# Three edits of an order in an encoder layer: feature casts of the first FFN step put later, an event for each half of the residual's spill, eleven dummy matmuls

## The chip, the cores and the metric

The kernel runs on one core of one Trainium2 chip. The metric is the device time of one execution in microseconds; the time before is the median of three runs. One further execution was taken with the hardware profiler, and all readings of the trace are from that one.

## The reference, cut to what matters

One encoder layer over 256 tokens of width 2048. What bears on the change is the middle of it:

```python
h  = h + rms_norm(mixed, g_mix_post)
fn = rms_norm(h, g_ffn_pre)
ff = (silu(fn @ w_ffn_gate) * (fn @ w_ffn_up)) @ w_ffn_down      # 2048 -> 5632 -> 2048
h  = h + rms_norm(ff, g_ffn_post)
gate = sigmoid(rms_norm(h, g_ple_pre) @ w_ple_gate)
h  = h + rms_norm(gate * (p @ w_ple_proj), g_ple_post)
```

Ahead of it stand one input projection, neighbourhood attention for half of the columns, a two-way recurrence for the other half, and an output projection.

## The kernel before, in words

**Products.** Each float32 operand is split into a high part (a cast to a reduced type) and a low part (the operand less its high part), and a product is three matmuls: high by high, low by high, high by low. A weight tile is 256 rows by 512 columns, one load of 512 KB into a raw tile (`wr`, `third`, `lower`). ScalarE casts it to `wh` (line 630), VectorE writes `wl` as the difference (line 643), and TensorE then runs twelve matmuls with the pair (lines 677 to 679). There are four `wh`/`wl` pairs in a ring (`W_BUFS = 4`), and in the FFN every fifth tile has a pair of its own, named `w`. A cast into a ring pair has to wait until TensorE is done with the tile that was there four ring casts earlier.

**FFN.** The 5632 columns are done in eleven steps `f` of 512, in three parts. In a step, the products with `w_ffn_gate` and `w_ffn_up` are formed (nine steps of the eleven, and most down products, do part of them with seven block products in place of eight, which needs sums of weight blocks made on VectorE at lines 578, 582 and 588, and one accumulating load on GpSimd's queue at line 599). `gate_post` writes silu of the gate to `mid`; `up_post` multiplies by the up product, transposes blocks on VectorE (line 334), and `moved` turns the tile by 16 small transfers `mT<-mid` (line 344). When these have landed, `carried` splits `mT` into the features `mid0h` and `mid0l` (lines 306 and 308) that the down products will read, and `mid_sums` makes block differences of `mT` in place (line 1761) and splits them into `sums`. The first step's features are first read after four steps.

**Combination.** When a group's seven block products are done, `made_of_four` joins them: a copy `u<-acc` on ScalarE (line 736), four subtractions on VectorE (lines 738 to 745), a copy `acc<-u` on ScalarE (line 730). The next group's matmuls add to these accumulators and wait for it.

**Residual.** `h` lies in two tiles of 1 MB, one for each half of the tokens. Once the FFN's input features exist, `spill_h` stores both to memory, so that their room can hold other tiles (`lower` in the first half's, `sums` in the second half's), and `reload` brings them back near the end.

**Order.** Every engine works through its instructions in the order in which they are written. That order comes from a planner at build time: each piece of side work is a generator that yields operations with an estimated cost. The planner keeps an estimated clock for each engine and takes, between the matmuls, the operation that can start first, with a lateness added or taken off. `plan.add(gen, ready, late)` starts a generator at the estimated time `ready`; an `Event` that a generator yields holds it until the estimated time of `done(event)`, which is `plan.now`. A new estimate moves instructions only where it changes which operation is taken first.

**Start.** `WARM` dummy matmuls of 128 columns on a tile of ones run on TensorE ahead of the first product (line 2101). Each is two records in the trace.

Of the kernel before, what the change touches and what calls it, by code (L numbers as in the profile page):

```python
# [18 lines left out]
NT = S // P  # L19
# [50 lines left out]
SOON = 2.0  # L70
ADDED = 6.0
AHEAD = 5
ISSUE = 160
WARM = 9


class Event:


    t = None  # L80
# [141 lines left out]
def dve(n, take=None, give=None):  # L222
    return ("dve", COST["dve"] + 0.00104 * n, None, take, give)
# [6 lines left out]
def dma(kb, take=None):  # L230
    return ("dma", kb / 340.0, None, take, None)
# [3 lines left out]
def layer(ctx: ExitStack, tc: tile.TileContext, a: dict, out: bass.AP):  # L235
# [5 lines left out]
    plan = Plan(wr=R_BUFS, w=W_BUFS, sm=SM_BUFS, acc=4, ev=1, mid=2, bt=2, m2=1, mt=1, sq=1, T0=1, T1=1, T4=1, **{f"{s}{j}": n for s, m, n in (("p", 5, 1), ("t", 3, 0)) for j in range(m)}, wr0=1, w0=1)  # L241
# [4 lines left out]
    def bank(name):  # L246
        return ps.tile([P, 2, S], F32, tag="sm", name=name, bufs=SM_BUFS)
# [55 lines left out]
    def split(hi, lo, src, n, give=None):  # L303

        yield act(n)
        nc.scalar.copy(hi, src)
        yield dve(n, give=give)
        nc.vector.tensor_tensor(out=lo, in0=src, in1=f32(hi), op=ALU.subtract)
# [19 lines left out]
    def moved(e, here, take, tile_of, turn=True, pool=()):  # L328


        if turn:
            flat = e.rearrange("p t n -> p (t n)")
            yield dve(2 * N)
            nc.vector.transpose(out=flat, in_=flat)
        src = e.rearrange("p t (k j b) -> p t k j b", j=4, b=32)
        mT = None
        for j in range(4):
            for i in range(4):
                first = None if mT else take
                yield ("pool" if i in pool else "dma", COST["move"], None, first, None)  # L340
                if mT is None:
                    mT = tile_of()
                dst = mT.rearrange("p t k (i b) -> p t k i b", b=32)
                (nc.gpsimd if i in pool else nc.sync).dma_start(  # L344
                    dst[32 * j : 32 * j + 32, :, :, i, :],
                    src[32 * i : 32 * i + 32, :, :, j, :],
                )
        done(here)
        return mT.rearrange("p t k q -> p k t q")

    def by_tile(v):
        return v.rearrange("p k (t q) -> p k t q", t=NT)
# [13 lines left out]
    def done(event):  # L366
        event.t = plan.now
# [438 lines left out]
    ev_unmerged = Event()  # L806
# [709 lines left out]
    def next_norm(sub, nxt, rstd, ev_rstd, g_next):  # L1516
# [51 lines left out]
        if sub is mix:  # L1568
            plan.add(spill_h(), plan.now)
# [28 lines left out]
        ).tile([NT, P, D], F32, name=f"part{i}")  # L1598
        for i in range(2)
    ]  # L1600
    ev_spilled, ev_back = Event(), Event()

    def spill_h():
        for e in hF.ev:
            yield e
        for t in range(NT):
            yield dma(1024)
            nc.sync.dma_start(spill[t], t2["h"].tiles[t])
        done(ev_spilled)

    half_spill = ctx.enter_context(
        tc.tile_pool(name="half_spill", bufs=1, space=bass.MemoryType.DRAM)
# [106 lines left out]
    def up_post(f, mid, kk0, g, soon):  # L1719

        def post(ch):
            yield g.free
            e = es.pop(f)
            for t in range(NT):
                yield dve(N)
                nc.vector.scalar_tensor_tensor(
                    out=e[:, t, :], in0=ch.accs[t], scalar=rstd_f[:, t : t + 1], in1=e[:, t, :],
                    op0=ALU.mult, op1=ALU.mult,
                )
            ch.release()  # L1730
            there = Event()
            mT = yield from moved(e, there, "mt", mT_tile, pool=(0, 2) if soon else range(4))
            plan.free["mid"].append(plan.now)
            yield there
            plan.add(carried(mid, kk0, mT), plan.now + (0.5 if soon else 3.0), -SOON if soon else 0.0)
        return post

    def carried(mid, kk0, mT):
        summed = any(kk0 <= kx < kk0 + 4 for kx in mid.ev_sums)
        for b in range(0, 4, 2):  # L1740
            kk = kk0 + b
            i, j = divmod(kk, 8)
            hi, lo = mid.tiles(i)
            yield from split(
                *(by_tile(x[:, j : j + 2, :]) for x in (hi, lo)), mT[:, b : b + 2], 2 * S,
                give="mt" if b and not summed else None,
            )
            mid.pair(kk)
        if summed:
            plan.add(mid_sums(mid, kk0, mT), plan.now + (20.0 if mid.name[-1] == str(2) else 0.0))  # L1750

    def mid_sums(mid, kk0, mT):

        yield ev_unmerged if kk0 else ev_spilled
        kxs = [kx for kx in DOWN_KS[2] if kk0 <= kx < kk0 + 4]
        m = 2 * len(kxs)
        a11, a12 = mT[:, 0:m:2, 0, :], mT[:, 1:m:2, 0, :]
        a21, a22 = mT[:, 0:m:2, 1, :], mT[:, 1:m:2, 1, :]
        for dst, x, y in ((a22, a21, a22), (a21, a21, a11), (a11, a11, a22), (a12, a12, a11)):
            yield dve(P * len(kxs))  # L1760
            nc.vector.tensor_tensor(out=dst, in0=x, in1=y, op=ALU.subtract)
        if kk0 == 0:
            if "sums" not in t2:
                t2["sums"] = t2["pool"].tile([P, 2, 4, S], F32R, tag="h1", name="sums")
            hi, lo = (by_tile(t2["sums"][:, i, :, :]) for i in range(2))
        else:
            hi, lo = (
                by_tile(t2["s"][:, 2 + i, :].rearrange("p (k s) -> p k s", s=S)) for i in range(2)
            )
        yield from split(hi, lo, mT[:, 0:m], m * S, give="mt")  # L1770
        for i, kx in enumerate(kxs):
            mid.sums[kx] = {
                n: tuple(x[:, 2 * i + k, t, :] for x in (hi, lo))
                for n, k, t in (("S2", 0, 0), ("S7", 0, 1), ("S4", 1, 0), ("S1", 1, 1))
            }
            done(mid.ev_sums[kx])
# [76 lines left out]
    for part, (f0, f1) in enumerate(PARTS):  # L1853
        mid = Mid(f"mid{part}")
# [243 lines left out]
    with tc.manual_schedule():  # L2098
        warm = bank("warm")
        for n in range(WARM):  # L2100
            nc.tensor.matmul(warm[:, 0, 0:P], ones, ones, start=True, stop=True)
# [90 lines left out]
```

## Time and profile before

| | |
|---|---|
| median of 3 runs | 1159.08 us (1156.46 to 1161.56) |
| the profiled execution's own time | 1159.04 us |
| its span, first to last instruction | 1157.1 us |
| TensorE busy | 1144.7 us (99% of the span) |
| VectorE, ScalarE, GpSimd busy | 903.7, 711.1, 133.5 us |
| mean granted TensorE clock | 0.997 |
| memory traffic | 222 GB/s over the span |

Times are in microseconds from the span's start unless marked ns. PE is TensorE, PEld its weight loads, DVE VectorE, ACT ScalarE, POOL GpSimd, SP SyncE, which issues most loads. A row of the timeline gives start, duration, engine, line, operation, output and inputs, count, and in brackets the engine's idle time before it and what ended that time. Ends of matmuls are modelled and overlap; the distance between two starts is the better measure of their pace. The granted clock is a share of full speed.

### The profile page before, as it was taken

What the parts mean: (1) busy time and instruction counts of PE and PEld (TensorE: products, weight loads), DVE (VectorE), ACT (ScalarE), POOL (GpSimd) and SP (SyncE); (2) the same over time, 40 slices, a digit from 0 to 9 for tenths busy, and PEclk for the clock granted to TensorE, in tenths of its full rate; (3) what the DMA queues carried; (4) which work ended last, traced back from release to release, by engine and by line L of the source; (5) the groups of instructions that cost most, each with busy time, mean ns of one, the idle gap of its engine ahead of it and who ended that gap; (6) DMA issues with size and microseconds to landing.
All of it is one profiled execution on the core that took longest, in us unless ns stands there. A gap on an engine that the chain in (4) does not pass through costs nothing.

```text
span 1157.1 us, 15105 instructions
## 1 busy us (share of the span) xinstructions
PE 1144.7 (99%) x5213; PEld 949.7 (82%) x5213; DVE 903.7 (78%) x1133; ACT 711.1 (61%) x944; POOL 133.5 (12%) x214
## 2 busy tenths in 40 slices
PE   9999999999999989999999999999999999999997
PEld 8888888888888878888888888888888888787886
DVE  6678787888468758898877898978878887868575
ACT  7777777875557545565555556555455564655664
POOL 0000000000000032131110133212111303100000
PEclk9999999999999999999999999999999999999999
DMA  9867666545686977877876877776987787875671
GB/s 323 286 186 226 183 180 206 179 158 200 224 283 189 307 197 260 241 228 231 249 246 219 261 220 216 258 246 205 316 260 252 217 265 241 271 239 198 221 247 75
DMA packets 112285, 266.39 MB, mean 230 GB/s; under 512 B 39248, under 2 KB 46160, under 8 KB 110800
## 3 DMA queue, kind: packets, MB, share of 16 engines
q1 hardware_dynamic: 99568, 243.57, 61.9%
q0 software_dynamic: 12208, 21.51, 9.5%
q8 instruction: 41, 0.67, 0.2%
q10 hardware_dynamic: 432, 0.35, 0.1%
q14 instruction: 36, 0.29, 0.1%
HBM read 247.55 MB, written 9.44 MB: 222 GB/s over the span
## 4 chain that ended last, share of the span: by engine, by line
PE 93%; DMA 3%; DVE 1%; ACT 1%; POOL 1%; issue 1%; ACTq 0%; DVEq 0%
PE acc L678 24%; PE acc L679 24%; PE acc L677 24%; PE acc L690 5%; PE acc L689 5%; PE acc L688 5%; DMA mT<-mid 3%; PE tr L325 1%; POOL mT L344 1%; DMA wr<-in_w_ffn_gate 1%; DVE wl L643 0%; PE pg L356 0%; PE pg L357 0%; PE pg L355 0%; DVE h L1548 0%
## 5 line engine op out<-in xcount | busy, mean ns | idle before, releaser
L643 DVE TENSOR_TENSOR wl<-wr,wh 128x1024 fp32r<-128x1024 f32 (+1 forms) x309 | 369.7, 1210 | 117.0 <-ACT wh L630 113.5
L630 ACT CAST wh<-wr 128x1024 fp32r<-128x1024 f32 (+1 forms) x309 | 320.3, 1043 | 197.0 <-PE acc L678 142.7
L678 PE MATMUL acc<-wh,hT_mix_lo 128*128 128x512 f32 x400 | 155.8, 390 | 0.3 <-DVE hT_mix_lo L314 0.3
L677 PE MATMUL acc<-wh,hT_mix_hi 128*128 128x512 f32 x400 | 155.9, 390 | 0.0
L679 PE MATMUL acc<-wl,hT_mix_hi 128*128 128x512 f32 x400 | 155.6, 389 | 0.0
L344 POOL DMA_DIRECT2D mT<-mid x152 | 89.4, 599 | 555.3 <-DMA wr<-in_w_ffn_gate 400.9
L679 PE MATMUL acc<-wl,hT_hi 128*128 128x512 f32 x320 | 124.5, 390 | 0.0
L677 PE MATMUL acc<-wh,hT_hi 128*128 128x512 f32 x316 | 124.4, 394 | 0.0
L678 PE MATMUL acc<-wh,hT_lo 128*128 128x512 f32 x316 | 123.1, 390 | 0.0
L630 ACT CAST wh<-ple 128x1024 fp32r<-128x1024 f32 (+1 forms) x57 | 56.4, 992 | 76.4 <-DVE ple L582 42.9
L678 PEld LDWEIGHTS acc<-wh,hT_mix_lo 128*128 128x128 f32 x400 | 75.1, 188 | 16.5 <-DVE hT_mix_lo L314 1.0
L679 PEld LDWEIGHTS acc<-wl,hT_mix_hi 128*128 128x128 f32 x400 | 75.1, 188 | 15.6
L677 PEld LDWEIGHTS acc<-wh,hT_mix_hi 128*128 128x128 f32 x400 | 75.1, 188 | 15.5
L643 DVE TENSOR_TENSOR wl<-ple,wh 128x1024 fp32r<-128x1024 f32 (+1 forms) x57 | 65.3, 1147 | 13.0 <-ACT wh L630 12.5
L679 PEld LDWEIGHTS acc<-wl,hT_hi 128*128 128x128 f32 x320 | 60.1, 188 | 12.9
L678 PEld LDWEIGHTS acc<-wh,hT_lo 128*128 128x128 f32 x316 | 59.4, 188 | 11.5
L677 PEld LDWEIGHTS acc<-wh,hT_hi 128*128 128x128 f32 x316 | 59.4, 188 | 11.5
L599 POOL DMA_DIRECT2D ple<-in_w_ffn_up x27 | 24.0, 890 | 172.5 <-DVE wl L643 124.6
L643 DVE TENSOR_TENSOR wl<-third,wh 128x1024 fp32r<-128x1024 f32 x31 | 37.8, 1219 | 5.5 <-ACT wh L630 5.5
L630 ACT CAST wh<-third 128x1024 fp32r<-128x1024 f32 x31 | 32.6, 1051 | 14.8 <-PE acc L678 10.0
L678 PE MATMUL acc<-wh,hT_ffn_lo 128*128 128x512 f32 x104 | 40.8, 393 | 0.5 <-DVE hT_ffn_lo L314 0.5
L677 PE MATMUL acc<-wh,hT_ffn_hi 128*128 128x512 f32 x104 | 40.8, 392 | 0.0
(439 smaller groups left out, 2457.3 us busy)
## 6 DMA issues: line engine op xcount, KB each, us to landing
wr<-in_w_ffn_gate SPq DMA_DIRECT2D x78, 512.0 KB, 5.5
wr<-in_w_in SPq DMA_DIRECT2D x77, 512.0 KB, 4.4
wr<-in_w_ffn_down SPq DMA_DIRECT2D x62, 512.0 KB, 5.5
wr<-in_w_ffn_up SPq DMA_DIRECT2D x48, 512.0 KB, 5.2
wr<-in_w_out SPq DMA_DIRECT2D x32, 512.0 KB, 4.3
wr<-in_w_ple_gate SPq DMA_DIRECT2D x32, 512.0 KB, 4.5
lower<-in_w_ffn_up SPq DMA_DIRECT2D x22, 512.0 KB, 6.2
third<-in_w_ffn_down SPq DMA_DIRECT2D x14, 512.0 KB, 5.4
```

The lines of the kernel that those rows point to most:

```text
L325: nc.tensor.transpose(tr[:, b, t * P : (t + 1) * P], e[:, t, sl], ident)
L344: (nc.gpsimd if i in pool else nc.sync).dma_start(dst[32 * j : 32 * j + 32, :, :, i, :], src[32 * i : 32 * i + 32, :, :, j, :],)
L599: nc.gpsimd.dma_start(dst, src, accum_op=ALU.add)
L630: nc.scalar.copy(his[i][:, 0 : src.shape[1], :] if n == 2 else his[i][:, j, :], src)
L643: nc.vector.tensor_tensor(out=los[i][:, m, :], in0=src, in1=f32(his[i][:, m, :]), op=ALU.subtract)
L677: nc.tensor.matmul(accs[t], hi[:, sl], his[i][:, j, :], start=st, stop=False, **group)
L678: nc.tensor.matmul(accs[t], lo[:, sl], his[i][:, j, :], start=False, stop=False, **group)
L679: nc.tensor.matmul(accs[t], hi[:, sl], los[i][:, j, :], start=False, stop=sp, **group)
L688: nc.tensor.matmul(dst, x[0], wh, start=start, stop=False, skip_group_check=seeded)
L689: nc.tensor.matmul(dst, x[1], wh, start=False, stop=False, skip_group_check=seeded)
L690: nc.tensor.matmul(dst, x[0], wl, start=False, stop=stop, skip_group_check=seeded)
```

## The change

Three edits. The 12.0 stands for the first FFN step only (`f` is 0); the other steps keep 3.0, and the last step of a part 0.5. `ev_spilled` now becomes done at the first half's spill, and `ev_all_spilled`, for which the first step's `mid_sums` waits, at the second's.

```diff
-WARM = 9
+WARM = 11
...
     def spill_h():
         for e in hF.ev:
             yield e
-        for t in range(NT):
+        for t, ev in enumerate((ev_spilled, ev_all_spilled)):
             yield dma(1024)
             nc.sync.dma_start(spill[t], t2["h"].tiles[t])
-        done(ev_spilled)
+            done(ev)
+            plan.now += 40.0 if t == 0 else 0.0
...
-            plan.add(carried(mid, kk0, mT), plan.now + (0.5 if soon else 3.0), -SOON if soon else 0.0)
+            plan.add(carried(mid, kk0, mT), plan.now + (0.5 if soon else 3.0 if f else 12.0), -SOON if soon else 0.0)
...
-        yield ev_unmerged if kk0 else ev_spilled
+        yield ev_unmerged if kk0 else ev_all_spilled
```

ScalarE's order in the second FFN step, where the first step's features `mid0h` and `sums` are made between casts of weight tiles; before:

```order
L630 CAST w<-wr 128x1024
L630 CAST wh<-third 128x1024
L306 CAST mid0h_3779<-mT 128x512 x2
L630 CAST wh<-ple 128x1024
L630 CAST wh<-wr 128x1024 x2
L630 CAST w<-wr 128x1024
L306 CAST sums<-mT 128x1024
L630 CAST wh<-wr 128x1024
```

The same place of the same engine in the changed kernel:

```order
L630 CAST w<-wr 128x1024
L630 CAST wh<-third 128x1024
L630 CAST wh<-ple 128x1024
L630 CAST wh<-wr 128x1024 x2
L630 CAST w<-wr 128x1024
L630 CAST wh<-wr 128x1024
L306 CAST mid0h_3781<-mT 128x512
L630 CAST wh<-third 128x1024
L306 CAST mid0h_3781<-mT 128x512
L630 CAST wh<-ple 128x1024
L306 CAST sums<-mT 128x1024
```

The first `mid0h` now stands behind five more weight casts, the second behind six, and `sums` behind three more. VectorE's order moves with it.

ScalarE near the end of the third FFN step, where `u<-acc` and `acc<-u` are the combination's copies; before:

```order
L630 CAST wh<-third 128x1024
L630 CAST wh<-wr 128x1024 x2
L736 COPY u<-acc_4194 128x512
L630 CAST wh<-wr 128x1024
L730 COPY acc_4195<-u 128x512
```

The same place of the same engine in the changed kernel:

```order
L630 CAST wh<-third 128x1024
L630 CAST wh<-wr 128x1024 x3
L736 COPY u<-acc_4194 128x512
L630 CAST w<-lower 128x1024
L730 COPY acc_4195<-u 128x512
```

One weight cast moved ahead of the first copy, and another now stands between the two. Near the end of the first pair of down products a cast likewise moves ahead of the first copy, and another stands between the two.

SyncE's queue around the two spills `h_spill<-h` in the changed kernel, between loads of FFN weights:

```order
L1608 DMA h_spill<-h_2882 128x2048
L555 DMA wr<-in_w_ffn_up 128x1024
L555 DMA wr<-in_w_ffn_gate 128x1024
L555 DMA wr<-in_w_ffn_up 128x1024
L555 DMA wr<-in_w_ffn_gate 128x1024
L555 DMA wr<-in_w_ffn_up 128x1024
L1608 DMA h_spill<-h_2883 128x2048
```

And before:

```order
L1608 DMA h_spill<-h_2880 128x2048
L555 DMA wr<-in_w_ffn_up 128x1024
L555 DMA wr<-in_w_ffn_gate 128x1024
L555 DMA wr<-in_w_ffn_up 128x1024
L555 DMA wr<-in_w_ffn_gate 128x1024
L555 DMA wr<-in_w_ffn_up 128x1024
L1608 DMA h_spill<-h_2881 128x2048
```

Nothing moved here but the numbers of the tiles: the second spill stands at its old place, five loads behind the first. The whole queues of SyncE and GpSimd are in the same order in both kernels, and so are TensorE's matmuls but for the two more dummies.

More of the change, by code (lines that the diff above doesn't have):

```diff
@@ L1600, in layer @@
     ]
-    ev_spilled, ev_back = Event(), Event()
+    ev_spilled, ev_all_spilled, ev_back = Event(), Event(), Event()
     def spill_h():
```

## The prediction

> **What bounds the kernel now.** I read the page first, then TensorE's waits, then the timeline of each engine at the place where the longest of these waits lies.
>
> ```profile
> span 1157.1 us, 15105 instructions
> ...
> PE 1144.7 (99%) x5213; PEld 949.7 (82%) x5213; DVE 903.7 (78%) x1133; ACT 711.1 (61%) x944; POOL 133.5 (12%) x214
> ```
>
> TensorE is busy for 99% of the span, so the kernel gets faster only where TensorE stops waiting, runs at a better clock, or does less. Idle time of another engine counts only if it reaches TensorE. In the view of the waits, TensorE's own are few:
>
> ```profile
> PE acc L688 <- ACT wh L630: 2.2, 1, 2.2
> PE final L2034 <- ACT diag L2032: 2.0, 1, 2.0
> PE acc L690 <- DVE wl L643: 1.3, 2, 0.8
> PE warm L2101 <- POOL ones L290: 1.1, 1, 1.1
> ```
>
> The second and the fourth are the end and the start of the program. The first, 2.2 us for a weight cast, and 0.8 of the third are one place in the second FFN step. Here is ScalarE's timeline there:
>
> ```profile
> 409.63 1.05 ACT L630 CAST wh<-wr 128x1024 fp32r<-128x1024 f32 x1 [1.67 <-PE acc L678]
> 412.35 1.05 ACT L630 CAST wh<-wr 128x1024 fp32r<-128x1024 f32 x1 [1.67 <-PE acc L678]
> ...
> 414.25 1.05 ACT L630 CAST wh<-third 128x1024 fp32r<-128x1024 f32 x1
> 424.40 1.14 ACT L306 CAST mid0h<-mT 128x512 fp32r<-128x512 f32 x2 [9.10 <-DMA mT<-mid]
> 427.18 1.04 ACT L630 CAST wh<-ple 128x1024 fp32r<-128x1024 f32 x1 [1.64 <-DVE ple L582]
> 428.44 1.99 ACT L630 CAST wh<-wr 128x1024 fp32r<-128x1024 f32 x2 [0.21 <-DVE wr L588]
> ```
>
> The first two rows are the healthy state: a cast follows TensorE's release of a pair, 2.72 us after the one before. Then ScalarE stands for 9.10 us in front of `mid0h`, because the small transfers of `mT` have not landed. No weight is cast from 415.30 to 427.18. VectorE, whose `mid0l` stands ahead of the sums for the next tile, is held too:
>
> ```profile
> 425.05 0.69 DVE L308 TENSOR_TENSOR mid0l<-mT,mid0h 128x512 fp32r<-128x512 f32 x1 [8.12 <-ACT mid0h L306]
> 425.66 0.69 DVE L578 TENSOR_TENSOR ple<-wr 128x512 f32<-128x512 f32 x1
> ...
> 428.19 0.42 DVE L1761 TENSOR_TENSOR mT<-mT 128x256 f32<-128x256 f32 x1
> 428.53 1.22 DVE L643 TENSOR_TENSOR wl<-ple,wh 128x1024 fp32r<-128x1024 f32 x1
> ```
>
> TensorE uses up the tiles that lie ready and then stops:
>
> ```profile
> 423.21 0.39 PE L677 MATMUL acc<-wh,hT_mix_hi 128*128 128x512 f32 x1
> ...
> 425.70 0.39 PE L679 MATMUL acc<-wl,hT_mix_hi 128*128 128x512 f32 x1
> 428.28 0.50 PE L688 MATMUL acc<-wh,sf 128*128 128x512 f32 x1 [2.19 <-ACT wh L630]
> 428.62 0.40 PE L689 MATMUL acc<-wh,sf 128*128 128x512 f32 x1
> 429.80 0.50 PE L690 MATMUL acc<-wl,sf 128*128 128x512 f32 x1 [0.79 <-DVE wl L643]
> ...
> 433.64 0.43 PE L690 MATMUL acc<-wl,sf 128*128 128x512 f32 x1
> 433.90 0.40 PE L677 MATMUL acc<-wh,hT_mix_hi 128*128 128x512 f32 x1
> ```
>
> The twelve starts from 423.21 to 425.70 are one tile: eleven distances in 2.49 us, 0.226 us each. At that pace the matmul after 425.70 would start at 425.93, and the one at line 677 behind twelve block products at 425.93 + 2.72 = 428.65. It starts at 433.90, so the place costs **5.25 us**, more than twice what the view of the waits shows. Its parts: 2.35 from 425.93 to 428.28; 0.11 because the first distance is 0.34; 0.95 because the second is 1.18; and 1.84 because ten matmuls from 429.80 to 433.90 take 4.10 in place of 2.26. The last part is the clock:
>
> ```profile
> 425.90:428.30 2.40, 0.21 (x2) 0.02 (x1) 2.37 (x5) 1.04 (x1) 0.00 (x0) 1.00 0.00 0
> 428.30:434.00 5.70, 4.91 (x13) 3.23 (x14) 5.63 (x8) 5.56 (x6) 0.93 (x1) 0.70 0.37 60
> ```
>
> In the view by stretches the last columns are granted clock, DMA share and GB/s: the clock is 0.70 after the wait.
>
> The Trainium skill ("TensorE: Matmul & The Clock Gate", Part 1) says that the rate halves after an idle window of about 3.4 us. Taken strictly, 2.35 us idle should not halve it, and the place would be worth 3.4 us, not 5.25; the row with 0.70 differs from that, and the row decides.
>
> **The change part by part.**
>
> *The feature casts.* The planner now starts them 9 us later, and the order puts the first `mid0h` behind five more weight casts: `ple`, `wr`, `wr`, `w`, `wr`. Does that suffice? Four of the five go to the ring of four, so the fourth takes the pair that `third` had. That tile was cast last before the stall and is the last that TensorE works off before it, until 425.93. So `mid0h` cannot come before about 425.93 + 1.05 = 427.0. `mT` landed at 424.40, so ScalarE will not wait for it, with 2.6 us to spare. When `mT` lands does not hang on the moved casts: GpSimd's order is unchanged, and its transfers were all issued before the stall bit:
>
> ```profile
> L344 POOL DMA_DIRECT2D mT<-mid x16: 582/588/1012, 402.7 to 416.7; - x16
> ...
> DMA to landing us min/median/max: 4.3/7.2/8.9
> ```
>
> Are the casts that go first ready? The next tile, `ple`, needs the sum at line 582, whose inputs are loads on SyncE. The last of these, and in the view of the transfers its time to landing, are
>
> ```profile
> 409.62 0.44 SPq L538 DMA_DIRECT2D lower<-in_w_ffn_up  x1
> ...
> lower<-in_w_ffn_up SPq DMA_DIRECT2D x1, 512.0 KB, 8.3
> ```
>
> so it lies there at about 418.4 (an estimate: 410.06 and 8.3). Then come 0.69 for the sum, 1.05 for the cast and 1.22 for `wl`: ready at 421.4, where TensorE wants it at 425.93. The cover is 4.5 us; without it each us late costs TensorE one, plus up to 1.84 for the clock. The two spills are issued before all this, and SyncE's loads, held behind tiles that VectorE had not worked off (no bytes at all moved from 425.9 to 428.3), now go on. So the whole 5.25 us should go.
>
> What is late next? Behind the landing of `mT` stand, on ScalarE, two casts `mid0h`, `third`, `ple` and `sums`; on VectorE two `mid0l`, two `wl`, four differences at line 1761, three sums of weights, `wl<-ple`, `sums`, another `wl`. With 0.62 for the first `mid0h`, 0.69, 0.42, 0.69 and 1.22 for the kinds on VectorE this is about 0.6 + 5 x 0.69 + 5 x 1.22 + 4 x 0.42 = 11.8 us (`sums` taken like a `wl`, which has its shape) until the second tile of the next block group is split. TensorE wants that one after five more tiles' worth and a half: 425.93 + 5.5 x 2.72 = 440.9. So a landing up to about 429 costs nothing; it was at 424.40, so 4.7 us are to spare. The slot that `mT` frees is next wanted at the end of the second step, some 14 us after `sums` can be done:
>
> ```profile
> 455.58 8.85 POOL L344 DMA_DIRECT2D mT<-mid  x15 [12.27 <-DVE mid L334]
> ```
>
> This place is worth **-5.25 us**, between -3.4 (if part of the stall comes back) and -5.3 (all of it, and the few distances of 0.23 behind it).
>
> *The spill.* In the planner a transfer's successor may start when the transfer does; the 40 us are added to `plan.now` behind `done(ev)` and overwritten at the next operation. The order on SyncE shows the second spill where it was. **0 us**, with nothing to hide it, as nothing moves; only an estimated time of an event changes.
>
> *The dummies.* They end right where the first product starts:
>
> ```profile
> 1.14 4.21 PE L2101 MATMUL warm<-ones 128*128 128x128 f32 x18 [1.14 <-POOL ones L290]
> ...
> 5.41 0.79 PE L669 MATMUL acc<-wh,hT_hi 128*128 128x512 f32 x1
> 6.00 0.63 PE L670 MATMUL acc<-wh,hT_lo 128*128 128x512 f32 x1
> 6.43 0.63 PE L669 MATMUL acc<-wh,hT_hi 128*128 128x512 f32 x1
> ...
> 7.64 0.39 PE L669 MATMUL acc<-wh,hT_hi 128*128 128x512 f32 x1
> 7.86 0.39 PE L670 MATMUL acc<-wh,hT_lo 128*128 128x512 f32 x1
> ```
>
> Eighteen records in 4.21 us are 0.234 each, so 22 last until 1.14 + 5.15 = 6.29, and the first product starts 0.88 us later. Not all of that is lost. Real matmuls go at 0.43 (6.00 to 6.43) until about 7.2, then at 0.22 (7.64 to 7.86), and one distance of 0.59 at the start is a wait for `hT_lo` that has time to go away. If the clock rises at the same moment, two slow matmuls (6.29, 6.72) and then fast ones from 7.15 bring the seventh product to 8.05, where it was at 7.64: **+0.4 us**. It is at least 0 (if the clock rises within the dummies, these run faster as well) and at most +0.88.
>
> The Trainium skill (the same page and part) says that the warm-up is a matter of time in a free-running window of about 3.4 us, not of a number of matmuls. By that rule the rise may lie 3.4 to 6.8 us behind the first dummy; the page gives no gain from dummies once products are ready, and the two extra ones cost 0 to about 0.45 us, with the +0.4 near its upper end.
>
> *The third step and the down products.* The combination there has a cast more in front of it:
>
> ```profile
> 488.54 0.59 ACT L736 COPY u<-acc 128x512 f32<-128x512 f32 x1 [1.17 <-PE acc L690]
> ...
> 490.67 0.59 ACT L730 COPY acc<-u 128x512 f32<-128x512 f32 x1 [0.60 <-DVE u L740]
> ```
>
> ScalarE is idle for 1.17 ahead of the first copy and for 0.60 ahead of the second, so 1.05 of a cast fits ahead of the first. Between them `w<-lower` has from 489.1, when the first copy ends, to 490.67, and runs 1.05 if its pair is free. **0 us**, up to +2 if one of these casts has to wait for its pair.
>
> Sum: 1159.04 - 5.25 + 0.4 = **1154.2 us**, for a span of 1152.3. The profiled execution lies 0.04 from the median of the three runs, 1159.08, so no more is to be allowed for than their spread, about 2.5 us to either side.
>
> **The rivals.** A difference of 0.5%, 5.8 us, is about what a measurement of this kernel can tell from none; the forecast, -4.9, is just short of it, and the line is at 1153.3.
>
> 1. *The stall is only partly there to win.* The three runs differ by 5.1 us, as much as the stall, and landings from 4.3 to 8.9 us suggest that it is not the same in each execution. If the median run has only its idle parts, 3.4, the result is 1159.1 - 3.4 + 0.4 = 1156.1. For: the spread. Against: the profiled time is the median.
> 2. *The features become the late part: slower.* If `mT` lands later because SyncE's loads no longer pause, ScalarE stands in front of `mid0h` with everything behind it, now nearer to TensorE's need. From a landing at 429 each us costs one, and the clock 1.84 more; from about 432 the gain is gone. At 438 it is 9 + 1.84 + 0.4 = 11.2 against 5.25, so 1165.0. Against: that is a landing 13 us later, and the slowest now takes 8.9.
> 3. *The copies of the combination wait behind casts.* Up to 2 us at one place: 1156.2. Against: the two idle times above.
> 4. *The change does not do what it says.* For the spill this is so by the order, and it is in the sum; for the casts the order shows the move.
>
> **How the numbers follow.** The forecast gets 0.72, rival 1 0.15, rival 2 0.06, rival 3 0.07. The forecast's own spread, 1152 to 1156.5, puts some four tenths of its chance below 1153.3: faster 0.30. Slower by over 0.5% is rival 2 and a mishap of rival 3 on top of a bad median: 0.06. The same: 0.64. The range goes from 1151.0 (all of the 5.3, no cost of the dummies, a median 2.8 lower than the sum) to 1158.0, which takes in rivals 1 and 3 with the runs' spread; it leaves out rival 2 and the tails.
>
> **What would show it.** Right: `mid0h` with no idle time for a DMA ahead of it, behind about 427 (less the shift of the start); no wait of TensorE at line 688 in the second step; granted clock 1.00 in that stretch; the dummies' 22 records to about 6.3 and the seventh product near 8.05; the second spill five loads behind the first. Wrong: a wait for `mT<-mid` behind 429, a TensorE wait for `wh` or `wl` some tiles later, a new wait ahead of line 677 behind a combination, or loads of weights that take clearly longer than 8.3 us.

## The result and the profile after

The changed kernel takes **1153.88 us** (median of 16 runs, 1153.12 to 1157.29) against 1159.87 (median of 16 runs, 1155.33 to 1161.98): a ratio of **0.9954**, 95% interval 0.9944 to 0.9965. The profiled execution took 1153.59 us, its span is 1151.6. The forecast was 1154.2. Like it, the median lies just short of half a per cent; the interval reaches across that line. The forecast added its -4.85 to 1159.04; the medians of these 16 runs each differ by 5.99, from a kernel before that is 0.8 slower than the three runs had it.

TensorE's waits in the changed kernel; the columns are engine and line, what it waited for, total, times, longest:

```profile
PE final L2035 <- ACT diag L2033: 2.0, 1, 2.0
PE warm L2102 <- POOL ones L290: 1.1, 1, 1.1
PE acc L678 <- DVE hT_ffn_lo L314: 0.5, 1, 0.5
...
PE acc L690 <- DVE wl L643: 0.2, 1, 0.2
```

The wait at line 688 is gone, and nothing of its size stands in its place. ScalarE's timeline at that point of the second step:

```profile
414.74 1.04 ACT L630 CAST wh<-third 128x1024 fp32r<-128x1024 f32 x1
419.41 1.05 ACT L630 CAST wh<-ple 128x1024 fp32r<-128x1024 f32 x1 [3.63 <-DVE ple L582]
420.37 1.99 ACT L630 CAST wh<-wr 128x1024 fp32r<-128x1024 f32 x2
423.71 1.05 ACT L630 CAST w<-wr 128x1024 fp32r<-128x1024 f32 x1 [1.35 <-PE acc L678]
426.43 1.05 ACT L630 CAST wh<-wr 128x1024 fp32r<-128x1024 f32 x1 [1.67 <-PE acc L678]
427.39 0.61 ACT L306 CAST mid0h<-mT 128x512 fp32r<-128x512 f32 x1
...
428.85 0.61 ACT L306 CAST mid0h<-mT 128x512 fp32r<-128x512 f32 x1
```

Between `third` and the first `mid0h` five weight casts run. ScalarE again waits for TensorE's release of a pair, 1.35 and 1.67 us, which is the healthy state, and `mid0h` no longer waits for a transfer. VectorE, with the two rows that the next tile needs and the split of `sums` later on, and TensorE, at the matmul that used to stand still:

```profile
418.61 0.69 DVE L582 TENSOR_TENSOR ple<-ple,lower 128x512 f32<-128x512 f32 x1 [0.59 <-DMA lower<-in_w_ffn_up]
...
420.49 1.22 DVE L643 TENSOR_TENSOR wl<-ple,wh 128x1024 fp32r<-128x1024 f32 x1 [0.59 <-ACT wh L630]
...
436.25 1.23 DVE L308 TENSOR_TENSOR sums<-mT,sums 128x1024 fp32r<-128x1024 f32 x1
```

```profile
426.19 0.39 PE L679 MATMUL acc<-wl,hT_mix_hi 128*128 128x512 f32 x1
426.42 0.39 PE L688 MATMUL acc<-wh,sf 128*128 128x512 f32 x1
```

The matmul at line 688 follows after 0.23 us, where it followed after 2.58. The two stretches that showed the slow clock before, in the view by stretches (last columns: granted clock, DMA share, GB/s):

```profile
425.90:428.30 2.40, 2.40 (x12) 1.97 (x12) 0.39 (x2) 1.87 (x3) 0.00 (x0) 1.00 1.04 404
428.30:434.00 5.70, 5.70 (x27) 4.73 (x26) 5.63 (x9) 1.33 (x3) 0.00 (x0) 1.00 0.85 304
```

TensorE is busy throughout, at clock 1.00, and loads flow at 404 GB/s where none moved.

To see where the 5.5 us of span come from, I took every distance between two starts on TensorE's timeline, subtracted the 0.227 us of full pace, and summed what is left over each place (kinds of matmul that run at another pace do so in both kernels and drop out). Before, the second step loses 5.22 us and after nothing; the start loses 0.37 more (seventh product at 8.01 for 7.64); the tenth step loses 0.86 for 1.38; one place near 1090 loses 0.18 for 0.34. That is -5.22 + 0.37 - 0.52 - 0.16 = -5.53. The last two were not in the forecast.

### The profile page after: what moved, and what is told of

The parts are those of the page before. It is cut to its first block, busy times and chain, and to the rows that moved or that the text cites. A ratio compares the mean times of both kernels' runs of the same rounds, so it can differ in the third digit from the quotient of the medians.

```text
span 1151.6 us, 15107 instructions
## 1 busy us (share of the span) xinstructions
PE 1142.6 (99%) x5217; PEld 949.8 (82%) x5217; DVE 904.0 (78%) x1133; ACT 710.8 (62%) x944; POOL 133.5 (12%) x214
## 4 chain that ended last, share of the span: by engine, by line
PE 96%; DVE 1%; DMA 1%; ACT 1%; POOL 0%; issue 0%; ACTq 0%; DVEq 0%; POOLq 0%
PE acc L679 25%; PE acc L678 25%; PE acc L677 25%; PE acc L690 5%; PE acc L688 5%; PE acc L689 5%; DMA mT<-mid 1%; PE tr L325 1%; PE warm L2102 0%; POOL mT L344 0%; PE pg L356 0%; PE pg L357 0%; PE pg L355 0%; DVE wl L643 0%; DVE h L1548 0%
```

## The experiments

The prediction's theory: the casts alone carry the gain, the dummies cost about 0.4, the spill edit does nothing. The rivals: one of the other edits moves the time too, or the gain depends on less or more of the move. Each diff is against the kernel before unless it says otherwise; places are compared by the loss defined above.

**The dummies alone.**

```diff
-WARM = 9
+WARM = 11
```

> The kernel before with eleven dummies for nine, nothing else. Theory (the casts carry the whole gain, the dummies cost a little): the dummies run at 0.214 us a record (22 records put the first product at 5.85 in the trace after), so the first product starts at 5.85 and the seventh at 8.0 where it was at 7.64, +0.4 us; the wait of ScalarE ahead of mid0h and TensorE's wait of 2.2 us at line 688 stay. About 1160.2 against 1159.8, a ratio of 1.000. Rival (the dummies carry part of the gain, by an earlier rise of the clock): the seventh product earlier than 7.64 and a ratio of 0.999 or less.

Measured: 1160.49 us, ratio 1.0005 (0.9996 to 1.0014). TensorE's start:

```profile
1.13 4.50 PE L2101 MATMUL warm<-ones 128*128 128x128 f32 x22 [1.13 <-POOL ones L290]
5.39 0.48 PE L669 MATMUL acc<-wh,hT_hi 128*128 128x512 f32 x1
...
6.86 0.39 PE L669 MATMUL acc<-wh,hT_hi 128*128 128x512 f32 x1
```

And the same in the changed kernel, with as many dummies:

```profile
1.14 5.07 PE L2102 MATMUL warm<-ones 128*128 128x128 f32 x22 [1.14 <-POOL ones L290]
5.85 0.77 PE L669 MATMUL acc<-wh,hT_hi 128*128 128x512 f32 x1
...
8.01 0.39 PE L669 MATMUL acc<-wh,hT_hi 128*128 128x512 f32 x1
```

The ratio came as expected, the seventh product did not: 6.86, not 8.0. With eleven dummies it starts at 6.86 in one execution and 8.01 in the other; with nine, between 6.90 and 7.72 in the ten executions of this case (7.64 before). The moment at which the pace doubles varies. In this execution it comes within the dummies: 22 records take 4.26 us up to the first product, and the products then run at nearly full pace, six distances in 1.47 us. In the changed kernel the dummies keep 0.214 us each, and the products too start slowly, six distances in 2.16 us. The view by stretches says 1.00 for the granted clock in the first 9 us of every trace, so this is read from the distances alone. The seventh product thus moves by 1.15 us with eleven dummies, which is more than two dummies last (four records, 0.86 us). So the 0.37 in the trace of the changed kernel is not their price: between nine and eleven no difference shows.

This execution also holds the stall of before: ScalarE idles 8.73 us ahead of `mid0h`, and the place loses 5.88 us.

**The casts alone.**

```diff
-... plan.now + (0.5 if soon else 3.0), ...
+... plan.now + (0.5 if soon else 3.0 if f else 12.0), ...
```

> The kernel before with the 12.0 for the first step alone; nine dummies, the spill as it was. Theory: the stall at line 688 of the second step goes, and nothing is paid at the start: the seventh product stays at 7.64, the span is 0.4 us below that of the full change, about 1151.2, ratio about 0.995. Rival (the spill's new event or the dummies are needed for the gain): part of the stall stays, span above 1153.

Measured: 1154.36 us, ratio 0.995 (0.9937 to 0.9964). On ScalarE:

```profile
425.86 1.05 ACT L630 CAST wh<-wr 128x1024 fp32r<-128x1024 f32 x1 [1.67 <-PE acc L678]
426.82 0.61 ACT L306 CAST mid0h<-mT 128x512 fp32r<-128x512 f32 x1
```

The whole gain is here: the interval nearly coincides with that of the full change. Every engine works in the same order in this trace as in that of the full change, but for the two dummies, so the spill edit moves nothing and the other two edits need not do anything.

**No dummies.** The changed kernel with

```diff
-WARM = 11
+WARM = 0
```

> The changed kernel with no dummies at all. Theory (the clock rises 3.4 to 6.8 us behind TensorE's first work, so the dummies buy the part of that which lies ahead of 5.4): the first product still starts at 5.35, the products run at 0.43 until about 9 to 12, the start costs 1 to 3 us more than with nine; ratio 0.9965 to 0.9975, where e2 has 0.995. Rival (the early products wait for loads anyway): within 0.5 us of e2.

Measured: 1156.43 us, ratio 0.9969 (0.9956 to 0.9981).

```profile
5.33 0.80 PE L669 MATMUL acc<-wh,hT_hi 128*128 128x512 f32 x1 [5.33 <-ACT wh L630]
...
8.05 0.58 PE L669 MATMUL acc<-wh,hT_hi 128*128 128x512 f32 x1
```

Without dummies the products go at 0.43 us behind the first, to about 8.5 and not to between 9 and 12 as expected, and the seventh starts at 8.05. The median is about 2 us above that of the casts alone, but the two intervals overlap between 0.9956 and 0.9964, and the traces show less at the start: the seventh product comes 0.88 later than the 7.17 of the casts alone, and of that 0.8 is left at 30 us. The rest of the 4.0 us between these two profiled spans (1155.8 and 1151.8) lies at the tenth step, 3.66 us lost against 0.89, and near 1090, 1.39 against 0.83, where the two kernels have the same order. So the dummies as such seem worth something under 1 us; two more of them do not show. The first product starts at 5.33 with no dummies at all: it is released by its weight cast.

**Only one cast ahead of the first `mid0h`.** The changed kernel with nine dummies and

```diff
-3.0 if f else 12.0
+3.0 if f else 7.5
```

> The changed kernel with nine dummies and 7.5 for 12.0: the first mid0h stands behind one more weight cast (ple) in place of five, the second behind two. ScalarE still waits some 4 us for mT. Theory (what counts is that the next tile's cast and sums go ahead of the wait; TensorE has a few us in hand): TensorE finds the ple tile ready at 425.9 and waits at most 1 us in all for the tile behind it, without a drop of the clock; span 1151.5 to 1152.5, ratio 0.995 to 0.996. Rival (ScalarE's wait itself is what costs, and only an order without it brings the gain): a stall of 2 us or more with a drop of the clock, span above 1154.

Measured: 1155.2 us, ratio 0.9961 (0.9948 to 0.9973), span 1152.6.

```profile
418.82 1.05 ACT L630 CAST wh<-ple 128x1024 fp32r<-128x1024 f32 x1 [3.35 <-DVE ple L582]
424.37 0.62 ACT L306 CAST mid0h<-mT 128x512 fp32r<-128x512 f32 x1 [4.50 <-DMA mT<-mid]
```

ScalarE still idles 4.50 us for the transfers, and TensorE hardly notices: the place loses 0.3 us. What counted was that the next tile, `ple`, its sums on VectorE and its cast, went ahead of the wait. The span lies 0.1 above what was expected; the mechanism held.

**Only the second `mid0h` behind casts.** With 6.0 in place of 12.0, ScalarE's order is `mid0h`, `ple`, `wr`, `mid0h`; nine dummies.

> The changed kernel with nine dummies and 6.0 for 12.0; the spill at its old place. The first mid0h stays ahead of the ple cast, the second moves behind ple and one wr. ScalarE still waits some 9 us for mT. Theory A (from the landing at 424.4, the ple cast at 424.9 to 426.0 and its wl until 427.2 or later, where TensorE wants it at 425.9): a stall of 1.5 to 2.5 us and no or a short drop of the clock, so half the gain, span 1153 to 1155. Theory B (the order within the group after the landing is all that counts): no stall, as in e3, span 1152.

Measured: 1156.91 us, ratio 0.9974 (0.9962 to 0.9985).

```profile
423.23 0.62 ACT L306 CAST mid0h<-mT 128x512 fp32r<-128x512 f32 x1 [8.47 <-DMA mT<-mid]
423.76 1.04 ACT L630 CAST wh<-ple 128x1024 fp32r<-128x1024 f32 x1
```

and on VectorE, ahead of the landing:

```profile
417.03 0.69 DVE L582 TENSOR_TENSOR ple<-ple,lower 128x512 f32<-128x512 f32 x1
```

`ple` now waits for the landing, but not also for VectorE's first `mid0l` and the two sums that stood behind it before: VectorE makes the sums ahead of the features here. The place loses 1.39 us, nearly all of it idle time, with no slow matmul. By its ratio the kernel keeps about half of the gain, as theory A said; the profiled execution, 1154.68, is the fastest of the six, so the 1.39 need not be typical. So in these two executions most of the 5.22 us were not the wait for the landing itself but what was queued behind it, and the clock that fell.

**The casts later still.** With 25.0 in place of 12.0, nine dummies.

> The changed kernel with nine dummies and 25.0 for 12.0: both mid0h go behind ten and eleven more weight casts, sums behind the combination of the second step, so mT is given up some 15 us later. Theory (features are not needed for some 100 us; what they hold up is only the slot of mT): no stall at line 688, the second step's mT transfers start 2 to 4 us later, at most 1 us of a new wait; span 1151.5 to 1153, the same as e2. Rival 2 of the prediction in another form (late features are work nearer to TensorE's need): a stall of over 2 us at the second step's end or in the third, span above 1154.

Measured: 1157.65 us, ratio 0.9979 (0.997 to 0.9988): more than half of the gain is lost. There is no stall in the old place. `sums` moves to 453.74, and GpSimd's next step needs the slot of `mT` that `sums` gives up; first the changed kernel, then this one:

```profile
451.11 8.70 POOL L344 DMA_DIRECT2D mT<-mid  x15 [13.67 <-DVE mid L334]
```

```profile
456.34 5.85 POOL L344 DMA_DIRECT2D mT<-mid  x10 [21.77 <-DVE sums L308]
```

```profile
475.56 1.14 ACT L306 CAST mid0h<-mT 128x512 fp32r<-128x512 f32 x2 [5.92 <-DMA mT<-mid]
```

The second step's transfers start 5.2 us later, released by `sums` and not by their data, and land late, so that a smaller stall of the same kind comes one step on: 1.91 us are lost at 477. Another 1.01 are lost at 450, ahead of these transfers, where TensorE waits for a `wl` that VectorE splits behind other work; what put it late there was not tried. My theory of at most 1 us fell, and the rival, that the features become the late part, is right here. Of the delays tried, 12.0 is the best: at 6.0 the landing of `mT` still holds up the next tile, at 25.0 the slot of `mT` is given up too late.

**A spill that is really later.** The 40 us in the change are overwritten. Here the generator waits for an event instead:

```diff
+            done(ev)
+            if t == 0:
+                wait = Event()
+                wait.t = plan.now + 40.0
+                yield wait
```

It is issued at 433.28 where it was at 394.77. This moves `ple` between the two `mid0h` as well.

> The kernel before (nine dummies, 3.0 for the first step) with the second half's spill truly 40 us later in the planner's time: an event with that time is yielded between the two spills, and on SyncE's queue the second spill stands 23 loads behind the first in place of five. The order of the feature casts changes by one place (a weight cast comes between the two of them). Theory (mT lands late because of its own transfers, not because of the spill): mT still lands at 423 to 425, ScalarE waits 8 to 9 us ahead of mid0h, TensorE stalls at line 688; span 1155.5 to 1157.5, a ratio of 0.998 to 1.000. Rival (1 MB written just ahead of the mT transfers is what makes them late): mT lands 2 to 3 us earlier, the stall shrinks by as much, and the spill done right would be worth half the gain, ratio about 0.997.

Measured: 1156.5 us, ratio 0.9973 (0.9961 to 0.9984).

```profile
423.77 0.62 ACT L306 CAST mid0h<-mT 128x512 fp32r<-128x512 f32 x1 [6.35 <-DMA mT<-mid]
...
444.36 1.05 ACT L306 CAST sums<-mT 128x1024 fp32r<-128x1024 f32 x1 [4.36 <-DMA h_spill<-h]
```

My theory failed: there is no stall at line 688. But two things had changed, so the same spill was run with both `mid0h` held ahead of `ple`, by 1.5 in place of 3.0 for the first step:

> The kernel before with the second spill truly later (as in e3), and 1.5 for 3.0 as the first step's delay, which keeps both mid0h ahead of the ple cast as before (only sums moves, by two casts). e3 showed no stall at line 688, against my theory there; it had the late spill and one cast between the two mid0h. Theory A (the spill just ahead of the mT transfers makes them late, as seen from TensorE's progress by 2.8 us): the stall at line 688 shrinks from 5.2 to about 1 to 2.5 us with nothing else changed at mid0h; span 1153 to 1155. Theory B (the cast between was what helped): the stall stays at 4 to 5 us, span 1156 to 1157.5.

Measured: 1157.86 us, ratio 0.9984 (0.9974 to 0.9995).

```profile
424.20 1.14 ACT L306 CAST mid0h<-mT 128x512 fp32r<-128x512 f32 x2 [8.20 <-DMA mT<-mid]
...
445.07 1.05 ACT L306 CAST sums<-mT 128x1024 fp32r<-128x1024 f32 x1 [4.05 <-DMA h_spill<-h]
```

and on TensorE:

```profile
426.41 0.39 PE L679 MATMUL acc<-wl,hT_mix_hi 128*128 128x512 f32 x1
428.09 0.50 PE L688 MATMUL acc<-wh,sf 128*128 128x512 f32 x1 [1.29 <-ACT wh L630]
428.42 0.40 PE L689 MATMUL acc<-wh,sf 128*128 128x512 f32 x1
429.35 0.50 PE L690 MATMUL acc<-wl,sf 128*128 128x512 f32 x1 [0.53 <-DVE wl L643]
429.69 0.39 PE L688 MATMUL acc<-wh,sf 128*128 128x512 f32 x1
```

The stall is back but loses 2.37 us in place of 5.22, as theory A said: the two idle pieces are 1.15 us shorter together (1.45 and 0.70 for 2.35 and 0.95), and the matmuls behind them keep full pace, which is worth the rest. The late spill gives 1.32 back near 450, because `sums` lies in the room that the spill has to clear. The span that was expected was missed, mainly by that loss and by 3.9 us at 1091; the profiled execution, 1161.62, is the slowest of the eleven. `mT` does land earlier with the spill out of the way, but not by the 2.8 us that the expectation took from TensorE's progress: the last of its sixteen transfers lands 6.36, 7.22 and 7.13 us behind its issue in the three traces with the late spill, and 7.71 to 8.53 us in the ten with the early one. In the kernel with `ple` between, TensorE itself was 2.1 us later at this place than before, mostly from delays at the start and near 212, and the last transfer was issued only 0.7 later; that hides a part of the stall too.

**The real spill and the casts together**, with nine dummies:

> All of the change as its words say it, with nine dummies: the 12.0, and the second spill truly 40 us later (23 loads behind the first, as in e3 and e5). Theory (the late spill saved 2.8 us of landing, which e2 no longer needs, and makes sums wait for its own landing, 4.4 us in e3): no gain over e2, a wait of ScalarE ahead of sums for the spill and about 0.5 to 1.5 us lost near 450; ratio 0.995 to 0.9965. Rival (the two gains add): span below 1151, ratio below 0.994.

Measured: 1154.83 us, ratio 0.9961 (0.9947 to 0.9975).

```profile
438.44 1.05 ACT L306 CAST sums<-mT 128x1024 fp32r<-128x1024 f32 x1 [0.61 <-DMA h_spill<-h]
```

The gains do not add: once the casts are out of the way, an earlier landing is worth nothing. The loss near 450 that was expected did not come, since `sums` waits 0.61 us and not 4.

**The tenth step as well.** In the trace of the casts alone the same pattern stands there, with `ple` behind the features:

```profile
973.05 1.14 ACT L306 CAST mid2h<-mT 128x512 fp32r<-128x512 f32 x2 [5.58 <-DMA mT<-mid]
975.84 1.06 ACT L630 CAST wh<-ple 128x1024 fp32r<-128x1024 f32 x1 [1.64 <-DVE ple L582]
```

It loses 0.89 us. So, for nine dummies and the spill as it was:

```diff
-0.5 if soon else 3.0
+0.5 if soon else {0: 12.0, 9: 7.5}.get(f, 3.0)
```

> e2 (the 12.0 for the first step, nine dummies) and, at the tenth step's features, 7.5 for 3.0. There e2 shows the same picture on a small scale: ScalarE waits 5.58 us for mT ahead of mid2h, the ple cast behind it comes late, and TensorE loses 0.9 us (up to 3.7 in e8). Theory: with the ple cast first the loss there goes to under 0.3 us; span about 0.7 us below e2, 1151.1, and over many runs a little more, ratio 0.9935 to 0.9945. Rival (as in e7: what is put later is wanted elsewhere, here by the combination's copies, one weight cast more being between them): a new wait of 0.5 us or more behind it, nothing won.

Measured: **1153.14 us**, ratio 0.9941 (0.9929 to 0.9954), as expected; the span, 1151.8, is no shorter than that of the casts alone, since the place near 1090 loses 1.89 us in this execution and 0.83 in that one.

```profile
972.11 1.05 ACT L630 CAST wh<-ple 128x1024 fp32r<-128x1024 f32 x1 [5.04 <-DVE ple L582]
973.06 0.62 ACT L306 CAST mid2h<-mT 128x512 fp32r<-128x512 f32 x1
```

The loss there is gone. It is the lowest median of all, though its interval overlaps those of the changed kernel and of the casts alone, so that the times do not show a gain. With 9.0 for 7.5:

> As e9 with 9.0 for 7.5: two weight casts go ahead of the first mid2h in place of one. Theory: the loss at the tenth step's place under 0.3 us, span as e9 within 0.5 us. Rival: the features come too late for the down products that follow, a new wait at line 677 or 678 on mid2l.

Measured: 1154.05 us, ratio 0.9955 (0.9942 to 0.9967). The place loses 1.06 us again, in a way that neither theory nor rival named: the two sides differ in where VectorE splits a tile `wr` among the combination's subtractions (lines 738 to 745). First with 7.5, where it stands between the first and the second of them:

```profile
980.38 1.22 DVE L643 TENSOR_TENSOR wl<-wr,wh 128x1024 fp32r<-128x1024 f32 x1
```

and with 9.0, where it stands behind all four, VectorE and TensorE:

```profile
982.71 2.35 DVE L643 TENSOR_TENSOR wl<-wr,wh 128x1024 fp32r<-128x1024 f32 x2
```

```profile
983.98 0.50 PE L679 MATMUL acc<-wl,hT_mix_hi 128*128 128x512 f32 x1 [0.79 <-DVE wl L643]
```

TensorE waits 0.79 us for that `wl`. So this move has its limit too, 1.5 us of estimated time further on.

## Why the prediction was right, step by step

**What bounds it.** Right. The stall was worth its whole 5.25, not the 2.2 or 3.4 of the idle times: 5.22 went, and the casts alone give 0.995, 5.7 us of 1160.1. The slow matmuls behind the wait belong to its price.

**The casts, -5.25.** Right in size and in each step. The first `mid0h` was to come not before 427.0; less the later start (`third` is cast 0.49 later) that is 427.5, and it came at 427.39. The next tile was to be ready at 421.4: `wl` ended at 420.49 + 1.22 = 421.71. The slot of `mT` was called free some 14 us early: `sums` is split by 436.25 + 1.23 = 437.48, the next transfers start at 451.11, 13.6 us on. What the prediction did not see is that this slack is also the limit in the other direction: with 25.0 it is used up. The margin for a landing as late as 429 was not tried.

**The spill, 0.** Right: the queue is unchanged, and the casts alone give the same orders and do as well as all three edits. Unexpected was that the idea behind the edit has a real side. Done truly, it shrinks the stall and makes `sums` wait 4 us instead; with the casts moved, neither matters.

**The dummies, +0.4.** The size in the trace is right (8.01 for 8.05 forecast), but by luck. The step that failed is "0.234 each": the 4.21 us of the group included the modelled end of the last record, and 22 records really went from 1.14 to 5.85, 0.214 each. "They end right where the first product starts" failed with it: the eighteen end earlier, and the first product waits for its weight cast, as in the kernel without dummies, where it starts at 5.33. And the pace does not change at a fixed moment, as the sum assumed. The Trainium skill ("TensorE: Matmul & The Clock Gate", Part 1) says that the window runs freely and that the count of slow matmuls varies from run to run; the seventh product between 6.86 and 8.01 with the same eleven dummies agrees. The range of 0 to 0.88 should have been taken as the answer, not its middle.

**What the sum left out.** -0.52 at the tenth step and -0.16 near 1090. With them the two spans differ by 5.5 and the medians by 6.0, where the sum had 4.85; that the time itself came within 0.3 us is luck in part, since the median before rose by 0.8. Both places vary between executions of kernels that do not differ there: the tenth step loses 0.86 here and 3.66 in the profiled execution without dummies, the place near 1090 loses 0.18 here and 3.9 in the one with the real spill alone. Such differences can make a good part of the runs' spread; whether they make all of it cannot be told, as one execution of each kernel has a trace.

**The rivals.** The first, that the median run holds only part of the stall, is refuted as far as two executions (5.22 and 5.88) and the casts' ratio go. The second, late features, did not happen at 12.0; at 25.0 it did, by the slot and not by the landing. The third, copies of the combination behind casts, did not happen in the third step; the tenth step with 9.0 shows the reverse, a weight tile's split behind the combination. The fourth held for the spill.

## What to carry to other kernels

Price a stall by the starts on both sides of it, not by the wait that the view names: here 2.2 us of wait were 5.2 us of time, through the work queued behind the waiting instruction and the slower clock after. One tile's sums and cast moved ahead of the wait removed nearly all of it; with the waiting instruction moved too far, it holds a buffer and makes a smaller stall one step later. Before a comment or a number in an order is believed, compare the orders: the 40 us of the spill moved nothing.

## What the runs showed of the hardware

Two short idle stretches close together can drop the clock. Idle of 2.35 and then 0.95 us within 4 us (before) gave ten matmuls in 4.10 us; in the kernel with eleven dummies alone 1.98 and 0.95 us gave a row of matmuls 0.43 apart:

```profile
427.62 0.50 PE L688 MATMUL acc<-wh,sf 128*128 128x512 f32 x1 [1.82 <-ACT wh L630]
...
429.73 0.63 PE L688 MATMUL acc<-wh,sf 128*128 128x512 f32 x1
430.15 0.63 PE L689 MATMUL acc<-wh,sf 128*128 128x512 f32 x1
```

With the real spill alone, 1.45 and 0.70 us did not: the matmul after 429.35 follows 0.34 later, and then 0.23. But the size of the two pieces sets no limit: in the kernel without dummies 1.14 and 0.69 us at the tenth step did drop the clock, to 0.50 in the view by stretches (granted clock third from the end):

```profile
979.25 0.50 PE L688 MATMUL acc<-wh,sums 128*128 128x512 f32 x1 [0.98 <-ACT wh L630]
...
980.51 0.50 PE L690 MATMUL acc<-wl,sums 128*128 128x512 f32 x1 [0.53 <-DVE wl L643]
```

```profile
977.83:981.23 3.40, 1.90 (x7) 0.95 (x7) 2.81 (x5) 3.08 (x4) 0.47 (x1) 1.00 1.02 424
981.25:984.64 3.39, 3.39 (x9) 2.58 (x9) 3.39 (x4) 2.81 (x4) 0.44 (x1) 0.50 0.79 189
```

The rule of the Trainium skill that the prediction cited, an idle window of about 3.4 us, would have forecast no drop in any of the four, if it means one unbroken idle time. Ahead of the program's end the thirteen traces hold four drops, and in the same view the clock is 0.50 for 3.4 us each time or twice that: from 430.3 to 433.7 before, from 428.2 to 435.0 with eleven dummies alone, from 981.2 to 984.6 without dummies and from 1094.6 to 1098.0 with the real spill alone. In the 3.4 us just ahead of each, TensorE is busy for 1.20, 1.58, 1.90 and 1.65 us, by the modelled ends. Counted back from the drop at 1094.55 in its own trace, in steps as long as that drop in the record of the clock (3.413 us), the 1.45 and 0.70 us fall into two stretches, busy for 1.99 and 3.01 us, and the clock stayed. This fits a count of busy time over fixed stretches of 3.4 us, so that the same idle time can cost the clock or not by where it falls; five cases do not prove it, and no run varied it.
